# Retention heads in a decoder step: small TensorE products joined in fewer runs

## The chip, the cores and the metric

The kernel runs on one core of one Trainium2 chip, in one launch. The metric is the time of the whole launch on the device, in microseconds (us), as the median of several executions. The engines named are TensorE (PE, the matrix products; PEld is its weight load), VectorE (DVE), ScalarE (ACT), GpSimd (POOL) and SyncE (SP, which here only issues DMAs). Each runs its own program in a fixed order; semaphores make one wait for another.

## The reference, cut to what matters

One inference step of a decoder with two layers, for 512 prompt tokens and for 8 sample sequences of 4 tokens with stored states. Layer 0 is a short gated convolution, layer 1 a multi-scale retention, each followed by a gated MLP. The change lies in layer 1 alone:

```python
def step(S, qkv):
    qc, kc, vc = qkv
    scores = jnp.einsum('bhid,bhjd->bhij', qc, kc) * decay
    inner = jnp.einsum('bhij,bhjv->bhiv', scores, vc)
    cross = jnp.einsum('bhid,bhdv->bhiv', qc, S) * cross_w[:, :, None]
    S_new = S * chunk_decay[:, None, None] + jnp.einsum('bhjd,bhjv->bhdv', kc * state_w[:, :, None], vc)
    return S_new, inner + cross
...
of = (of - mu) * lax.rsqrt(var + GN_EPS)
of = of.transpose(0, 2, 1, 3).reshape(B, L, V_DIM) * gn_g.astype(jnp.float32)
out = (jax.nn.silu(g) * of.astype(x.dtype)) @ w_out
```

There are four heads, with 256 key columns and 512 value columns each. So a head has q, k (rotated) and v by projection, for the prompt and for the 32 sample tokens; the prompt's output in four tiles of 128 tokens; the samples' output, which reads a 256 x 512 state of each of the 8 sequences and writes it back updated; a normalisation over the 512 values; a gate; and an output projection.

## The kernel before, in words

Everything is in float32. A large product is made of three: each factor is split in a high and a low part (`wh`, `wl`; `xh`, `xl`), and high x high, high x low and low x high are summed in PSUM. `mm3` (L175 to L177) does this for the products of a head, `project` (L187) for projections with 272-column halves, and L1272 to L1274 for the value projection ("V products"). PSUM is handed out as two kinds of tiles: `psum()` gives one of two double banks (tag `mm`), `bank()` one of four single banks (tag `sm`). A tile that is still being read holds up the next owner of its place.

A loop over the four heads (L1575 to L1662, h = 0 to 3) does, for each head:

- `value`: 96 V products into four `sm` banks, and at two points the sample tokens' values (L1280) into the first bank of an `mm` tile, `pvs[:, 0]`. At the first of these points stand also `sample_scores` (L1462, two products of 32 columns; in head 0 one more, L1459, that turns a mask) and `keys`: eight transposes of key tiles (L1331) and two transposes of the samples' keys (L1340). Each of these three takes a `psum()` of its own. At the end of `value` the second bank, `pvs[:, 1]`, gets a product with a placing matrix (L1309).
- `state` and `scores` for the prompt, and in between `fill(n)`: pieces of the output projection of the head before (`held_project`, 48 or 24 products of L187 at a time), put there so that TensorE has work. Head 0 has none.
- `sample_outputs(i)` for the four groups i = 0 to 3: four products of 8 columns (L1493), one for each pair of sequences, that read the state tile S[i] and add into one `sm` bank, `st["po"]`. The profile shows each product as two records.
- `states_update(i)`: four products of 32 rows (L1511) into two `mm` tiles, then DVE's S update (L1516, two halves), then the store of S[i] on SP (L1518).
- `inner(it)` for the four prompt tiles it = 0 to 3 (3 to 12 `mm3` products each), and behind it `normalized`: statistics on DVE (L1404, L1405, L245/L247), a power on POOL (L248), and the normalised tile `yn` on DVE (L1408).
- `gated`: four transposes of a `yn` (L1432, on TensorE) and a multiplication of the gate by the result (L1438; L1442 for the samples, `yns`, which come from `po`). `gated_pair` does two tiles in one `mm` tile.
- `qk_project`: q and k of the next head (48 products of L187 each). In its second half, `inside()` puts update 3 and the transposes of tile 2. In head 3 a piece of `held_project` takes its place.

The order of each engine's program is made by a scheduler from the program's order and its dependencies; `tc.issue_after(x)` adds the condition that what is issued inside comes after x. It is by such conditions that groups and updates are kept behind the last product named (`last_product`).

Of the kernel before, what the change touches and what calls it, by code (L numbers as in the profile page):

```python
# [52 lines left out]
def hybrid_decode_kernel(ctx: ExitStack, tc: tile.TileContext, a: dict, o: dict):  # L53
# [1072 lines left out]
    with ExitStack() as c2:  # L1126
# [50 lines left out]
        def token_tiles(tt):  # L1177
            return slice(tt * P, (tt + 1) * P)
# [81 lines left out]
        def value(h, st):  # L1260

            pv = [bank() for _ in range(4)]
            pvs = psum()
            raw = []
            for c in range(4):
                wh, wl = load_piece(a["rtv"][h, c], 2 * DV, keep=raw)
                for k2 in range(2):
                    kt = 2 * c + k2
                    cw = slice(k2 * DV, (k2 + 1) * DV)
                    for tt in range(4):  # L1270
                        ts_, out = token_tiles(tt), pv[tt]
                        nc.tensor.matmul(out, xh[kt][:, ts_], wh[:, cw], start=(kt == 0), stop=False)  # L1272
                        nc.tensor.matmul(out, xh[kt][:, ts_], wl[:, cw], start=False, stop=False)  # L1273
                        last = nc.tensor.matmul(out, xl[kt][:, ts_], wh[:, cw], start=False, stop=(kt == KT - 1))  # L1274
                if c % 2:

                    with tc.issue_after(last.ins):
                        for g in range(4):
                            kt = 2 * c - 2 + g
                            nc.tensor.matmul(  # L1280
                                pvs[g * NS : (g + 1) * NS, 0, :], xs[:, kt, :],
                                raw[kt // 2][:, kt % 2 * DV : (kt % 2 + 1) * DV],
                                start=(c == 1), stop=(c == 3), skip_group_check=True,
                            )
                if c == 1:
                    qk_split(h, st, 1)
                    qk_split(h, st, 0)
                    gs = st["gs"] = one.tile([P, NS], F32, tag="gs", name=nm("gs"), bufs=1)
                    nc.vector.tensor_mul(
                        by_sequence(gs), by_sequence(R[:, 1, HT - NS :]), fq[:, h, :].unsqueeze(1).to_broadcast([P, NB, DS])  # L1290
                    )
                    sample_scores(h, st)
                    for dt in range(2):
                        qsrc = st["rot"][0][:, dt, SEQ:].rearrange("p (g r s) -> p g r s", g=4, r=2)
                        for r in range(2):
                            nc.vector.scalar_tensor_tensor(
                                qm[:, dt, :, r, 4 * r : 4 * r + 4], qsrc[:, :, r, :], _gamma(h) ** 4,
                                gs.rearrange("p (g r s) -> p g r s", g=4, r=2)[:, :, r, :], op0=ALU.mult, op1=ALU.mult,
                            )
                    keys(h, st)  # L1300
                    if h in AHEAD:
                        held_parts(h, older)
            v4 = tp.tile([P, 2, DV], F32R, tag="mid", name=nm("v4"), bufs=1)
            nc.scalar.activation(v4[:, 0, :], pvs[:, 0, :], AF.Copy, scale=fv[:, 4, h : h + 1])
            nc.vector.scalar_tensor_tensor(
                v4[:, 1, :], pvs[:, 0, :], fv[:, 4, h : h + 1], v4[:, 0, :].bitcast(F32), op0=ALU.mult, op1=ALU.subtract
            )
            for i in range(2):
                nc.tensor.matmul(pvs[:, 1, :], put, v4[:, i, :], start=(i == 0), stop=(i == 1))  # L1309
            vt = kp.tile([P, DV], F32R, tag="rt0", name=nm("vt"), bufs=1)  # L1310
            vs = st["vs"] = qp.tile([P, DV], F32R, tag="vs", name=nm("vs"), bufs=1)
# [12 lines left out]
            st["v"] = (vh, vl)  # L1324

        def keys(h, st):
            krot = st["rot"][1]
            pt = psum()
            for jt in range(4):
                for dt in range(2):  # L1330
                    nc.tensor.transpose(  # L1331
                        pt[:, jt // 2, (jt % 2) * 256 + dt * P : (jt % 2) * 256 + (dt + 1) * P],
                        krot[:, dt, token_tiles(jt)], ident,
                    )
            knh = tp.tile([P, 2, 512], F32R, tag="skh", name=nm("knh"), bufs=1)
            knl = tp.tile([P, 2, 512], F32R, tag="skl", name=nm("knl"), bufs=1)
            split(knh, knl, pt)
            pt = psum()
            for dt in range(2):
                nc.tensor.transpose(pt[:, 0, token_tiles(dt)], kpl[:, dt].rearrange("p g q c -> p (g q c)"), ident)  # L1340
            kns = st["kns"] = tp.tile([P, 2, 2 * P], F32R, tag="kns", name=nm("kns"), bufs=1)
            kt = tp.tile([P, 2, 2 * P], F32R, tag="rt1", name=nm("kt"), bufs=1)
            for r in range(2):
                nc.scalar.activation(kt[:, r, :], pt[:, 0, : 2 * P], AF.Copy, scale=sign[:, 2 + r : 3 + r])
            for r in range(2):
                nc.vector.scalar_tensor_tensor(
                    kns[:, r, :], pt[:, 0, : 2 * P], low_k[:, r : r + 1], kt[:, r, :].bitcast(F32),
                    op0=ALU.mult, op1=ALU.add,
                )
            st["kn"] = (knh, knl)  # L1350
# [74 lines left out]
                )  # L1425
            return pt

        def gated(h, st, yn, it, pt=None):

            pt = bank() if pt is None else pt  # L1430
            for n in range(4):
                last_product[0] = nc.tensor.transpose(pt[:, token_tiles(n)], yn[:, token_tiles(n)], ident)  # L1432
            size = 4 // len(st["gate"])
            for i, gate in enumerate(st["gate"]):
                ps_ = pt[:, i * size * P : (i + 1) * size * P]
# [7 lines left out]

        def gated_pair(h, st, *pair):
            pt = psum()
            for i, (yn, it) in enumerate(pair):
                gated(h, st, yn, it, pt[:, i, :])

        def sample_scores(h, st):

            qrot, krot = st["rot"]
            pt = psum()
            for dt in range(2):
                nc.scalar.activation(
                    kpl[:, dt, :, :3, :],
                    krot[:, dt, SEQ:].rearrange("p (g c) -> p g c", g=4).unsqueeze(2).to_broadcast([P, 4, 3, 8]), AF.Copy,
                )
            if h == 0:
                nc.tensor.matmul(pt[:, 1, :NS], put[:NS].bitcast(F32), mask_s[:NS], start=True, stop=True)  # L1459
                nc.scalar.activation(mask_put, pt[:, 1, :NS], AF.Copy)  # L1460
            for dt in range(2):
                nc.tensor.matmul(  # L1462
                    pt[:, 0, :NS], kpl[:, dt].rearrange("p g q c -> p (g q c)"), qrot[:, dt, SEQ:],
                    start=(dt == 0), stop=(dt == 1),
                )
            ss = tp.tile([P, NS], F32, tag="ss", name=nm("ss"), bufs=1)
            nc.vector.tensor_mul(ss, pt[:, 0, :NS], mask_put)
# [12 lines left out]
            S = st["S"][i] = sp.tile([P, 4, DV], F32, tag="S", name=nm("S"))  # L1480
            st["loaded"] = nc.sync.dma_start(S, rets_in[r, h, dt])

        def sample_outputs(h, st, i):


            r, dt = RD[i]
# [1 line left out]
                st["po"] = bank()  # L1488
                nc.tensor.matmul(st["po"], scp, st["vs"], start=True, stop=False, skip_group_check=True)

            with tc.issue_after(last_product[0].ins):
                for g in range(4):
                    last_product[0] = nc.tensor.matmul(  # L1493
                        st["po"][32 * g : 32 * g + 8, :], qm[:, dt, g, r, :], st["S"][i][:, g, :],
# [80 lines left out]
        for h in range(NH):  # L1575
# [30 lines left out]
            states_update(h, st, 0)  # L1606
            states_load(h, st, 3)
            fill(3)
            if h in AHEAD:
                st["gate"] = [swapped(h == 2, [P, 4, T], F32, "gate")]  # L1610
            if more:
# [10 lines left out]
                for i, t in enumerate(st["gate"]):  # L1622
                    nc.sync.dma_start(t, gate_made[h][:, 2 * i : 2 * i + 2, :])
            yn0 = normalized(inner(h, st, 0), fe[:, 0, h : h + 1])
            sample_outputs(h, st, 1)
            yn1 = normalized(inner(h, st, 1), fe[:, 1, h : h + 1])
            states_update(h, st, 1)
            if more:

# [150 lines left out]
```

## Time and profile before

| | us |
|---|---|
| median of 3 runs | 1400.66 |
| lowest and highest of them | 1400.02 to 1401.79 |
| the profiled execution's own time | 1399.59 |
| its span, from first to last instruction | 1397.8 |

The granted clock of TensorE was 0.999 of full speed in the profiled execution. The retention heads stand between about 687 and 1002 us of the span. All durations below come from the profiled execution; the parts of a page are its head (busy time of each engine), the chain of work that ended last (each step followed back to what released it; in it a run of products of one line is one row, "x8" counts its records), the timeline (every instruction, with the idle time before it in brackets), and windows (busy time in a stretch). Products on TensorE overlap, so a row of the timeline is longer than the time between two starts; in the chain the rows add up to the time that passed.

### The profile page before, as it was taken

The numbers are of one execution on the slowest core, as the hardware profiler recorded it, in microseconds if no ns is written. First come the engines' busy times: TensorE is split into PE (matmuls) and PEld (weight loads), VectorE is DVE, ScalarE is ACT, GpSimd is POOL, SyncE is SP. The second block draws the span as 40 slices with busy tenths as digits, with TensorE's granted clock in tenths as the row PEclk, the third lists the DMA queues.
The fourth block names the chain that finished last, engine by engine and source line by source line (L and its number), as shares of the span: only waits on it lengthen the run. The fifth ranks groups of instructions, "written<-read, shape, count | busy, mean of one in ns | idle before, by whom it ended". The sixth has DMA issues, their size and how long they took to land.

```text
span 1397.8 us, 26508 instructions
## 1 busy us (share of the span) xinstructions
PE 1385.4 (99%) x10433; PEld 1314.1 (94%) x10433; DVE 1131.6 (81%) x1923; ACT 824.0 (59%) x1286; POOL 219.3 (16%) x255
## 2 busy tenths in 40 slices
PE   9999999999999999999999999999999999999997
PEld 9999999999999999999977877887899999999997
DVE  6987889898989879667867586586799898989884
ACT  7666467677667657667532314224387767677654
POOL 0111011222221214111200000000112212121212
PEclk9999999999999999999999999999999999999999
DMA  6466347768686744777667355465766877777742
GB/s 207 125 165 167 108 110 159 177 163 184 145 191 150 174 114 142 189 194 202 208 215 238 121 213 181 139 242 182 211 143 154 171 176 173 155 185 154 167 105 87
DMA packets 99294, 233.68 MB, mean 167 GB/s; under 512 B 9793, under 2 KB 33489, under 8 KB 98785
## 3 DMA queue, kind: packets, MB, share of 16 engines
q1 hardware_dynamic: 68032, 167.47, 38.4%
q0 software_dynamic: 28688, 56.61, 23.6%
q10 hardware_dynamic: 2448, 7.91, 1.5%
q8 instruction: 81, 1.33, 0.4%
q14 instruction: 45, 0.36, 0.1%
HBM read 191.84 MB, written 28.42 MB: 158 GB/s over the span
## 4 chain that ended last, share of the span: by engine, by line
PE 92%; DVE 4%; DMA 1%; issue 1%; ACT 1%; POOL 0%; SPq 0%; DVEq 0%; POOLq 0%; ACTq 0%
PE sm L389 43%; PE mm L389 16%; PE mm L187 14%; PE sm L187 4%; PE sm L1272 2%; PE sm L1274 2%; PE sm L1273 2%; PE sm L175 2%; PE sm L177 2%; PE sm L176 1%; PE sm L1493 1%; DMA w<-in_cvin_dram 1%; DVE S L1516 1%; PE mm L1280 1%; PE mm L1432 1%
## 5 line engine op out<-in xcount | busy, mean ns | idle before, releaser
L389 PE MATMUL sm<-oh,wh 128*128 128x272 f32 x856 | 247.8, 290 | 0.5 <-DVE b L450 0.5
L389 PE MATMUL sm<-ol,wh 128*128 128x272 f32 x856 | 246.1, 288 | 0.0
L389 PE MATMUL sm<-oh,wl 128*128 128x272 f32 x856 | 246.1, 287 | 0.0
L202 ACT ACTIVATE h<-w 128x1024 fp32r<-128x1024 f32 (+3 forms) x170 | 136.4, 803 | 94.6 <-PE mm L389 81.2
L203 DVE TENSOR_TENSOR l<-w,h 128x1024 fp32r<-128x1024 f32 (+3 forms) x170 | 153.6, 904 | 21.4 <-ACT h L202 19.4
L318 ACT ACTIVATE wh<-w 128x1024 fp32r<-128x1024 f32 (+1 forms) x134 | 133.9, 999 | 55.9 <-PE sm L389 47.7
L389 PEld LDWEIGHTS sm<-oh,wh 128*128 128x128 f32 x856 | 161.3, 188 | 2.0 <-DVE b L450 0.9
L389 PEld LDWEIGHTS sm<-oh,wl 128*128 128x128 f32 x856 | 161.0, 188 | 0.0
L389 PEld LDWEIGHTS sm<-ol,wh 128*128 128x128 f32 x856 | 160.8, 188 | 0.1
L389 PE MATMUL sm<-parts,wh 128*128 128x272 f32 x736 | 142.5, 288 | 0.0
L202 ACT ACTIVATE wh<-w 128x1024 fp32r<-128x1024 f32 (+3 forms) x76 | 68.1, 898 | 119.9 <-PE mm L187 61.4
L321 POOL DMA_DIRECT2D wl<-in_ffgu_dram x87 | 81.7, 939 | 323.1 <-ACT wl L320 97.4
L389 PEld LDWEIGHTS sm<-parts,wh 128*128 128x128 f32 x736 | 115.4, 188 | 0.0
L389 PE MATMUL mm<-oh,h 128*128 128x272 f32 x396 | 114.0, 288 | 0.0
L389 PE MATMUL mm<-oh,l 128*128 128x272 f32 x396 | 113.4, 286 | 0.0
L389 PE MATMUL mm<-ol,h 128*128 128x272 f32 x396 | 113.1, 286 | 0.0
L319 DVE TENSOR_TENSOR wl<-w,wh 128x512 fp32r<-128x512 f32 (+1 forms) x134 | 87.3, 652 | 25.0 <-ACT wh L318 24.7
L389 PE MATMUL sm<-parts,wl 128*128 128x272 f32 x368 | 106.2, 289 | 0.2 <-DMA wl<-in_rtqk_dram 0.2
L320 ACT ACTIVATE wl<-wh 128x512 fp32r<-128x512 f32 (+1 forms) x173 | 103.0, 595 | 2.2
L203 DVE TENSOR_TENSOR wl<-w,wh 128x1024 fp32r<-128x1024 f32 (+3 forms) x76 | 80.1, 1057 | 12.4 <-ACT wh L202 11.6
L187 PE MATMUL mm<-parts,wh 128*128 128x272 f32 x488 | 82.5, 290 | 0.2 <-ACT wh L202 0.2
L389 PE MATMUL sm<-oh,h 128*128 128x272 f32 x284 | 82.3, 290 | 0.2 <-ACT oh L202 0.2
(381 smaller groups left out, 3837.1 us busy)
## 6 DMA issues: line engine op xcount, KB each, us to landing
w<-in_ffgu_dram SPq DMA_DIRECT2D x66, 512.0 KB
wl<-in_ffgu_dram POOLq DMA_DIRECT2D x87, 256.0 KB, 5.3
S<-in_rets_dram SPq DMA_DIRECT2D x16, 1024.0 KB
out_rets_dram<-S SPq DMA_DIRECT2D x16, 1024.0 KB
w<-in_ffdn_dram SPq DMA_DIRECT2D x36, 384.0 KB
cb<-in_ffgu_dram SPq DMA_DIRECT2D x22, 512.0 KB
w<-in_cvin_dram SPq DMA_DIRECT2D x21, 512.0 KB
wl<-in_ffdn_dram POOLq DMA_DIRECT2D x48, 192.0 KB, 4.7
```

Of the source, the lines that this page charges most:

```text
L175: nc.tensor.matmul(out, lh, rh, start=start, stop=False, skip_group_check=True)
L177: last_product[0] = nc.tensor.matmul(out, ll, rh, start=False, stop=stop, skip_group_check=True)
L187: last_product[0] = nc.tensor.matmul(half(pt, hf)[:, :HT], w[:, c], act[k][:, hf * HT : (hf + 1) * HT], start=(first and k == ks[0] and i ...
L202: h = nc.scalar.activation(dh, src, AF.Copy)
L203: last_low[0] = nc.vector.tensor_sub(dl, src, dh.bitcast(F32))
L318: nc.scalar.activation(wh, w, AF.Copy)
L319: last_mixed[0] = nc.vector.tensor_sub(wl[:, :n], w[:, :n], wh[:, :n].bitcast(F32))
L320: nc.scalar.activation(wl[:, n:], wh[:, n:].bitcast(F32), AF.Copy, scale=-1.0)
L321: nc.gpsimd.dma_start(wl[:, n:], src[:, 1, :] if len(src.shape) == 3 else src[:, n:], accum_op=ALU.add)
L389: last = nc.tensor.matmul(out, w[:, c], b, start=(first and j == 0 and i == 0), stop=(j == len(self.ks) - 1 and i == 2), skip_group_check= ...
L1272: nc.tensor.matmul(out, xh[kt][:, ts_], wh[:, cw], start=(kt == 0), stop=False)
L1273: nc.tensor.matmul(out, xh[kt][:, ts_], wl[:, cw], start=False, stop=False)
```

## The change

It does five things, all in the retention heads.

1. `sample_scores` and the two key transposes of the samples no longer take a `psum()` each; they write `pvs[:, 1]`, the second bank of v's tile, which is free until L1309. The scheduler then puts them and the eight key transposes directly behind L1280.
2. `sample_outputs(1)` stands behind `inner(1)` in the code, and its products are ordered behind the last product of `fill(3)`.
3. `inside()` transposes tile 2 first and then does update 3.
4. `gated` is split in `over` (the transposes) and `through` (the gate's multiplications); `gated_pair` does the eight transposes back to back, the pair's second tile first.
5. With that, the first pair (tiles 0 and 1) stands directly ahead of group 3, and the last pair (samples and tile 3) stands 22 V products (head 1: 29) behind the start of the next head's V stream; before, the samples' transposes stood at its start and tile 3's 20 products later.

```diff
-                    sample_scores(h, st)
+                    sample_scores(h, st, pvs[:, 1, :])
...
-                    keys(h, st)
+                    keys(h, st, pvs[:, 1, P:])
...
-            pt = psum()
             for dt in range(2):
-                nc.tensor.transpose(pt[:, 0, token_tiles(dt)], kpl[:, dt].rearrange("p g q c -> p (g q c)"), ident)
+                nc.tensor.transpose(placed[:, token_tiles(dt)], kpl[:, dt].rearrange("p g q c -> p (g q c)"), ident)
...
-        def gated(h, st, yn, it, pt=None):
-
-            pt = bank() if pt is None else pt
+        def over(pt, yn):
+
             for n in range(4):
                 last_product[0] = nc.tensor.transpose(pt[:, token_tiles(n)], yn[:, token_tiles(n)], ident)
+
+        def gated(h, st, yn, it):
+
+            pt = bank()
+            over(pt, yn)
+            through(st, pt, it)
...
         def gated_pair(h, st, *pair):
             pt = psum()
-            for i, (yn, it) in enumerate(pair):
-                gated(h, st, yn, it, pt[:, i, :])
-
-        def sample_scores(h, st):
+            over(pt[:, 1, :], pair[1][0])
+            with tc.issue_after(last_product[0].ins):
+                over(pt[:, 0, :], pair[0][0])
+            for i, (_, it) in enumerate(pair):
+                through(st, pt[:, i, :], it)
+
+        def sample_scores(h, st, pt):
...
-        def sample_outputs(h, st, i):
+        def sample_outputs(h, st, i, behind=None):
...
-            with tc.issue_after(last_product[0].ins):
+            with tc.issue_after(last_product[0].ins), tc.issue_after((behind or last_product[0]).ins):
...
             fill(3)
+            filled = last_product[0]
...
             yn0 = normalized(inner(h, st, 0), fe[:, 0, h : h + 1])
-            sample_outputs(h, st, 1)
             yn1 = normalized(inner(h, st, 1), fe[:, 1, h : h + 1])
+            sample_outputs(h, st, 1, filled)
             states_update(h, st, 1)
...
             def inside():
+                gated(h, st, yn2, 2)
                 states_update(h, st, 3)
-                gated(h, st, yn2, 2)
```

Lines shift by up to 10 in the changed kernel: L1493 becomes L1502, L1511 L1520, L1432 L1430, L1462 L1471, L1340 L1339, L1408 L1407.

What it does to the programs of the engines is seen at three places. First, TensorE in the second head (h = 1), around the 48 held products of L187. Before, one product of group 1 stands ahead of them and three behind, and update 1 with group 2 stands six products further on:

```order
L177 MATMUL sm_9726<-vh_9380,sl_9551 128x512
L1493 MATMUL sm_9646<-S_9392,qm 8x512
L187 MATMUL mm_9669<-oldh_9300,wh_9664 128x272 x2
...
L187 MATMUL mm_9695<-oldh_9301,wl_9665 128x272 x2
L1493 MATMUL sm_9646<-S_9392,qm 8x512 x3
L175 MATMUL sm_9743<-vh_9380,sh_9550 128x512
...
L177 MATMUL sm_9743<-vh_9380,sl_9551 128x512
L1511 MATMUL mm_9759<-vs_9377,kns_9294 128x512 x2
L1511 MATMUL mm_9760<-vs_9377,kns_9294 128x512 x2
L1493 MATMUL sm_9646<-S_9394,qm 8x512 x4
```

And now:

```order
L187 MATMUL mm_9691<-oldh_9297,wl_9661 128x272 x2
L175 MATMUL sm_9735<-vh_9376,sh_9546 128x512
L176 MATMUL sm_9735<-vl_9377,sh_9546 128x512
L177 MATMUL sm_9735<-vh_9376,sl_9547 128x512
L1502 MATMUL sm_9642<-S_9388,qm 8x512 x4
L1520 MATMUL mm_9755<-vs_9373,kns_9290 128x512 x2
L1520 MATMUL mm_9756<-vs_9373,kns_9290 128x512 x2
L1502 MATMUL sm_9642<-S_9390,qm 8x512 x4
L175 MATMUL sm_9776<-mid_9452,qkhl_9256 128x512
```

Group 1 is whole and stands with update 1 and group 2 in one run. Second, TensorE in the second head's V stream, at the first of the two points in `value`. Before:

```order
L1280 MATMUL mm_9190<-w_9221,xs 32x512 x2
L1462 MATMUL mm_9263<-rot_8908,kpl 128x32 x2
L1272 MATMUL sm_9186<-wh_9308,parts 128x512
L1273 MATMUL sm_9186<-wl_9309,parts 128x512
L1331 MATMUL mm_9278<-cb,rot_8909 128x128 x8
L1274 MATMUL sm_9186<-wh_9308,parts 128x512
...
L1272 MATMUL sm_9186<-wh_9308,parts 128x512
L1340 MATMUL mm_9291<-cb,kpl 128x128 x2
L1273 MATMUL sm_9186<-wl_9309,parts 128x512
```

And now, all of it in one run and on two `mm` tiles where there were four:

```order
L1280 MATMUL mm_9188<-w_9219,xs 32x512 x2
L1471 MATMUL mm_9188<-rot_8906,kpl 128x32 x2
L1331 MATMUL mm_9275<-cb,rot_8907 128x128 x8
L1339 MATMUL mm_9188<-cb,kpl 128x128 x2
L1272 MATMUL sm_9184<-wh_9304,parts 128x512
```

In the first head L1468 (before L1459) and three of the eight transposes stand ahead of L1471. Third, TensorE in the middle of the first head's second projection (`inside()`). Before:

```order
L187 MATMUL sm_9096<-parts,wl_9091 128x272
L1511 MATMUL mm_9121<-vs_8794,kns_8718 128x512 x2
L1511 MATMUL mm_9122<-vs_8794,kns_8718 128x512 x2
L187 MATMUL sm_9095<-parts,wh_9090 128x272
L1432 MATMUL sm_9130<-cb,yn_9069 128x128 x4
L187 MATMUL sm_9096<-parts,wh_9090 128x272
```

And now:

```order
L187 MATMUL sm_9094<-parts,wl_9089 128x272
L1430 MATMUL sm_9119<-cb,yn_9067 128x128 x4
L1520 MATMUL mm_9125<-vs_8792,kns_8716 128x512 x2
L1520 MATMUL mm_9126<-vs_8792,kns_8716 128x512 x2
L187 MATMUL sm_9093<-parts,wh_9088 128x272
```

The transposes stand first and touch the update. On DVE, in the same head, the samples' statistics now stand ahead of a weight split, their normalised tile ahead of the second half of update 2, and the normalised tile 3 behind update 3 as before. On SP only the second head's order differs: the gate's load stands ahead of the load of state tile 3 and of the next head's rotary load, where it stood behind both.

More of the change, by code (lines that the diff above doesn't have):

```diff
@@ L1324, in value, with keys @@
             st["v"] = (vh, vl)
-        def keys(h, st):
+        def keys(h, st, placed):
             krot = st["rot"][1]
@@ L1343, in keys @@
             for r in range(2):
-                nc.scalar.activation(kt[:, r, :], pt[:, 0, : 2 * P], AF.Copy, scale=sign[:, 2 + r : 3 + r])
+                nc.scalar.activation(kt[:, r, :], placed[:, : 2 * P], AF.Copy, scale=sign[:, 2 + r : 3 + r])
             for r in range(2):
                 nc.vector.scalar_tensor_tensor(
-                    kns[:, r, :], pt[:, 0, : 2 * P], low_k[:, r : r + 1], kt[:, r, :].bitcast(F32),
+                    kns[:, r, :], placed[:, : 2 * P], low_k[:, r : r + 1], kt[:, r, :].bitcast(F32),
                     op0=ALU.mult, op1=ALU.add,
@@ L1426, in inner, with through @@
             return pt
-        def gated(h, st, yn, it, pt=None):
-            pt = bank() if pt is None else pt
+        def over(pt, yn):
             for n in range(4):
                 last_product[0] = nc.tensor.transpose(pt[:, token_tiles(n)], yn[:, token_tiles(n)], ident)
+        def gated(h, st, yn, it):
+            pt = bank()
+            over(pt, yn)
+            through(st, pt, it)
+        def through(st, pt, it):
             size = 4 // len(st["gate"])
@@ L1445, in gated_pair @@
             pt = psum()
-            for i, (yn, it) in enumerate(pair):
-                gated(h, st, yn, it, pt[:, i, :])
-        def sample_scores(h, st):
+            over(pt[:, 1, :], pair[1][0])
[4 more added lines that the diff above has]
+        def sample_scores(h, st, pt):
             qrot, krot = st["rot"]
-            pt = psum()
             for dt in range(2):
@@ L1458, in sample_scores @@
             if h == 0:
-                nc.tensor.matmul(pt[:, 1, :NS], put[:NS].bitcast(F32), mask_s[:NS], start=True, stop=True)
-                nc.scalar.activation(mask_put, pt[:, 1, :NS], AF.Copy)
+                nc.tensor.matmul(pt[:, NS : 2 * NS], put[:NS].bitcast(F32), mask_s[:NS], start=True, stop=True)
+                nc.scalar.activation(mask_put, pt[:, NS : 2 * NS], AF.Copy)
             for dt in range(2):
                 nc.tensor.matmul(
-                    pt[:, 0, :NS], kpl[:, dt].rearrange("p g q c -> p (g q c)"), qrot[:, dt, SEQ:],
+                    pt[:, :NS], kpl[:, dt].rearrange("p g q c -> p (g q c)"), qrot[:, dt, SEQ:],
                     start=(dt == 0), stop=(dt == 1),
@@ L1466, in sample_scores @@
             ss = tp.tile([P, NS], F32, tag="ss", name=nm("ss"), bufs=1)
-            nc.vector.tensor_mul(ss, pt[:, 0, :NS], mask_put)
+            nc.vector.tensor_mul(ss, pt[:, :NS], mask_put)
             nc.vector.tensor_mul(ss, ss, st["gs"])
```

## The prediction

> **What bounds the kernel now.** I read the page's head first, then the shares of the chain that ended last.
>
> ```profile
> span 1397.8 us, 26508 instructions
> PE 1385.4 (99%) x10433; PEld 1314.1 (94%) x10433; DVE 1131.6 (81%) x1923; ACT 824.0 (59%) x1286; POOL 219.3 (16%) x255
> PE 92%; DVE 4%; DMA 1%; issue 1%; ACT 1%; POOL 0%; SPq 0%; DVEq 0%; POOLq 0%; ACTq 0%
> ```
>
> TensorE (PE) is busy for 1385.4 of 1397.8 us, and 92% of the chain is its own program. So there is almost no waiting to remove. A change in the order of TensorE's products can only pay if some product takes longer because of what stands before it. To see whether any does, I read the chain of waits where it runs through TensorE alone, in the second head. Its columns are the start in us, the duration in us, and the engine, PSUM kind and line.
>
> ```profile
> 807.83 0.95 PE sm L1493 x2
> 808.78 6.22 PE mm L187 x48
> 815.01 0.97 PE sm L1493 x6
> 815.98 0.43 PE sm L175
> ...
> 817.57 0.44 PE mm L1511 x3
> 818.01 0.97 PE sm L1493 x8
> 818.98 0.43 PE sm L175
> ...
> 821.26 6.02 PE mm L187 x48
> 827.29 0.44 PE mm L1432 x4
> 827.73 0.23 PE sm L175
> ...
> 828.87 0.48 PE mm L1432 x4
> 829.36 0.97 PE sm L1493 x8
> 830.33 0.43 PE sm L177
> ```
>
> Three things are to be seen. First, a group of L1493 takes 0.95 to 0.97 us whether 2, 6 or 8 records of it stand together (a product leaves two records, so 1, 3 or 4 products). A group cut in two is paid twice. Second, the first full product behind L1493 takes 0.43 where the same product elsewhere takes 0.23 (827.73). The same 0.20 stands on the 48 products of L187: 6.22 behind L1493, 6.02 behind a full product. So each separate run of such small products costs its own row and 0.20 behind it. Third, transposes (L1432) leave no such mark: 0.23 behind them. And where L1511 and L1493 stand together (817.57, 818.01), the second takes its usual 0.97 and the 0.20 comes once.
>
> The cut group appears in heads three and four as well; these are the second pieces:
>
> ```profile
> 904.29 0.97 PE sm L1493 x6
> 975.17 0.97 PE sm L1493 x6
> ```
>
> **Group 1 behind `inner(1)`.** In the second head the three runs now cost 0.95 + 0.20 (one product, then L187), 0.97 + 0.20 (three products) and 0.44 + 0.97 + 0.20 (update 1 with group 2), 3.93 together. Afterwards one run of group 1, update 1 and group 2 costs 0.97 + 0.44 + 0.97 + 0.20 = 2.58. That is 1.35 less, and 4.05 in heads two to four, where the group is cut. In the first head there is no held product and group 1 is whole; only its 0.20 goes. The sum is 4.25, all of it on TensorE's own chain. If joining saved nothing but the extra run, it would be 3 x (0.95 + 0.20) = 3.45; if each joint also hid some of the next group's start, perhaps 4.5. I take 4.25, since 817.57 to 818.98 shows such a joint at exactly this price. The move adds no operand that could be late: group 1 reads a state tile and a bank that its first product used 7 us sooner before (807.83 and 815.01). `inner(1)` now stands ahead of it, so DVE's statistics of that tile can start sooner; update 1 and its store start about 1.2 sooner too, since 0.95 + 0.20 went ahead of them.
>
> **Sample scores and key transposes in v's PSUM tile.** The chain in the second head's V stream:
>
> ```profile
> 762.97 0.99 PE mm L1280 x8
> 763.97 0.56 PE mm L1462 x4
> 764.53 0.32 PE sm L1272
> 764.85 0.24 PE sm L1273
> 765.08 0.87 PE mm L1331 x8
> ...
> 768.50 0.33 PE mm L1340 x2
> 768.83 0.24 PE sm L1273
> ```
>
> Before, L1280, L1462, L1331 and L1340 cost 0.99 + 0.56 + 0.87 + 0.33, and the V product behind L1462 costs 0.09 over 0.23: 2.84. Afterwards they are one run. The two last transposes go on at the pace of L1331 (0.87 / 8 = 0.11 each, 0.22 together), so the run is 0.99 + 0.56 + 0.87 + 0.22 = 2.64. That is 0.20 per head, 0.80 in four. In the first head L1459's product and the scores split the key transposes, two more joints of 0.09 each, so I take 0.6, with 0.1 and 0.8 as ends. A new wait comes with it: the key transposes of the samples now write the bank from which DVE reads the scores.
>
> ```profile
> 764.57 0.19 DVE L1467 TENSOR_TENSOR ss<-mm,mput 128x32 f32<-128x32 f32 x1 [4.42 <-PE mm L1462]
> ```
>
> DVE sat idle for 4.42 us before this read and did it in 0.19, so it is through about 0.25 after L1462, while the eight transposes between take 0.87. That covers it with 0.6 to spare. If DVE were still in other work then, what lies beyond the 0.6 would be paid by TensorE once per head, which is why the low end is 0.1.
>
> **Transposes of tile 2 ahead of update 3.** In the timeline and the chain of the first head:
>
> ```profile
> 742.85 0.51 PE L1511 MATMUL mm<-vs,kns 32*128 32x512 f32 x4
> 746.48 0.51 PE L1511 MATMUL mm<-vs,kns 32*128 32x512 f32 x4
> 747.47 0.66 PE L1432 MATMUL sm<-cb,yn 128*128 128x128 f32 x4 [0.15 <-DVE yn L1408]
> ...
> 742.92 0.49 PE mm L1511 x3
> 748.12 2.87 PE sm L187 x23
> ```
>
> From update 3's start to the 23 L187 behind the transposes it is 748.12 - 746.48 = 1.64, less 0.07 because the timeline starts this run 0.07 ahead of the chain (742.85 and 742.92): 1.57. Between them stands one L187 (2.87 / 23 = 0.125). Afterwards the same work is 0.48 for the transposes, 0.44 for the update, 0.20 behind it and 0.125: 1.25. The gain is 0.32, of which 0.15 is the wait for DVE's normalised samples. It needs that tile (which frees the bank the transposes write) to come earlier too, and the order on DVE does that: its statistics now stand ahead of a weight split and it stands ahead of the second half of update 2. Three heads give 0.96; the ends are 0.5 (the wait stays) and 1.4 (it also falls in heads two and three by more). In the fourth head this place lies on a chain through DVE, where I take 0:
>
> ```profile
> 997.87 0.82 DVE yn L1408
> 998.73 0.67 PE mm L1432 x4
> ```
>
> TensorE waits there for the last normalised tile whichever way the transposes ahead stand.
>
> **Pairs of transposed tiles.** First pair: before, 0.44 + 0.48 + 0.97 + 0.20 for two sets of transposes with five products between and group 3 (827.29 to 830.33). Afterwards the same rows in one run. Transposes leave no mark, so 0; the first head, whose second set took 0.1 longer, gives 0.1. Last pair: before, the samples' transposes stood at the head of the next V stream and tile 3's 20 products later, and now all eight stand 22 (second head: 29) products into it. The run is 0.88 either way. But TensorE now waits with everything behind it for both tiles, and tile 3's comes late:
>
> ```profile
> 754.92 0.81 DVE L1408 TENSOR_SCALAR yn<-sm,mv,rs 128x512 f32<-128x512 f32 x1 [0.52 <-POOL rs L248]
> 756.05 0.44 PE mm L1432 x4
> 700.00:1000.00 300.00, 299.26 (x1847) 236.73 (x1848) 211.47 (x340) 85.26 (x119) 12.21 (x21) 1.00 0.56 193
> 738.00:756.00 18.00, 17.85 (x113) 13.96 (x112) 17.14 (x30) 4.29 (x5) 1.62 (x3) 1.00 0.76 258
> ```
>
> The two last rows are windows: stretch and length, then the busy time of PE, PEld, DVE, ACT and POOL, the granted clock, the DMA share and GB/s. DVE is busy for 17.14 of the 18 us up to this place, so tile 3 is set by DVE's program. It ended at 755.7, 0.3 ahead of the transposes at 756.05. In the new order TensorE comes there at about 756.05 - 0.44 (the samples' transposes, no longer ahead) + 2 x 0.23 (two more V products) - 0.4 (tile 2 and the first pair, above) = 755.7, on the same scale, just when DVE ends. I price the whole at -0.3, with +0.1 and -1.0 as ends (0.25 in each of four heads, a third of one 0.81 DVE pass).
>
> **Moved transfers.** Only the second head's SP order differs: the gate load stands ahead of the load of state tile 3.
>
> ```profile
> 814.16 0.38 SPq L1481 DMA_DIRECT2D S<-in_rets_dram  x1
> 812.00:832.00 20.00, 20.00 (x133) 15.04 (x132) 16.05 (x26) 3.52 (x5) 1.08 (x2) 1.00 0.71 268
> ```
>
> The load is issued at 814.16 and its group starts at 829.36, 15.2 later, about 14 in the new order. The store ahead of it, the gate and the tile are 3.2 MB, 12 us at the window's 268 GB/s: hidden, so 0. If the cover were gone the group would wait up to the gate's own 1.1 MB, 4 us, so this part has an end at -1 (a quarter of it). The rotary load, one place later, feeds DVE and no product for some us.
>
> **The sum.** 4.25 + 0.6 + 0.96 + 0.1 - 0.3 = 5.6. The profiled execution took 1399.59, its span and 1.8 around it; it would take 1394.0. It lies 1.07 below the median of the runs, 1400.66, so the predicted median is 1395.1. A difference within 0.2% (2.8 us) can hardly be told from none.
>
> **The rivals.** *The joints keep their price* (0.15). Each change between full products, 8-column products and 32-row products costs what it does now, wherever it stands, and only the second piece of a cut group disappears: 3.45 from three heads, less 0.0 to 0.3 elsewhere, so about 1397.2. For it speaks that the 0.20 is seen at the end of runs only, so that what happens inside one is inferred; against it 818.01, where L1493 right behind L1511 takes no longer than behind full products. [...]
>
> *The gain is eaten by waits, no change* (0.09). Tile 3 comes some 0.8 late in each head, one DVE pass, and the scores' read costs 0.3 a head: 5.6 + 0.3 - 4 x 0.8 - 4 x 0.3 = 1.5, so 1399.2.
>
> *Slower* (0.06). The place is the joined last pair. All eight transposes and the V products behind them wait for the last pass of a DVE that is 95% busy (17.14 of 18). Without this part the gain is 5.9. It is used up when tile 3 comes 1.5 after TensorE in each of four heads, and the kernel is slower by more than 0.2% from 2.2 on. If three more passes like L1408 (0.81) came ahead of it, 2.4 late, it would be 1400.66 - 5.9 + 4 x 2.4 = 1404.4. Against it: DVE's program holds no new operation, its statistics move forward, and the two V products more add 0.46 of cover.
>
> **How the numbers follow.** The forecast gets 0.70; all its terms are rows of TensorE's own chain but for the last pair. Its own ends: with the upper ends 4.5 + 0.8 + 1.4 + 0.1 + 0.1 = 6.9, 1393.8; with the lower ends of the small parts, 4.25 + 0.1 + 0.5 - 1.0 = 3.85, 1396.8. The range takes in the first rival and 1 us of scatter at either end (the three runs shown lie from 0.6 below to 1.1 above their median): 1392.8 to 1398.3. Faster: 0.70 + 0.15 = 0.85. Same: 0.09. Slower: 0.06.
>
> **What would show it.** Right for group 1: in the second head one unbroken run of 0.97, 0.44 and 0.97 behind `inner(1)`, 0.43 on the product behind it, no L1493 beside the held L187, which take 6.02. Wrong: more than 0.97 on the second of them, or 0.20 more in between. Scores: L1280 to L1339 in about 2.65; wrong if the last two transposes name DVE's read as what they waited for. Tile 2: no idle time before L1430 inside the query projection. Last pair: no idle time over 0.3 before its eight transposes. What makes the forecast wrong most easily is TensorE idle there, on DVE's last pass, in all four heads.

## The result, and the profile after

The changed kernel takes 1399.78 us (median of 14 runs, 1397.85 to 1401.79), beside 1400.19 us for the kernel before, also in 14 runs. The ratio is 0.9994, with a 95% interval of 0.9987 to 1.0000: no difference that this measurement can tell. Forecast were 1395.1 and a range that ends at 1398.3.

The head of the changed kernel's page, and the waits of TensorE in the retention heads (in us: in total, times, longest):

```profile
span 1399.0 us, 26533 instructions
PE 1384.0 (99%) x10433; PEld 1317.1 (94%) x10433; DVE 1130.1 (81%) x1923; ACT 824.0 (59%) x1286; POOL 224.5 (16%) x255
```

```profile
PE sm L1502 <- DMA S<-in_rets_dram: 2.1, 1, 2.1
PE mm L1430 <- DVE yn L1407: 0.4, 1, 0.4
PE mm L1520 <- DVE gate L1445: 0.2, 1, 0.2
```

TensorE waited 0.5 us here before, now 2.7, and the largest part is new: group 3 of some head waits for its state tile.

This profiled execution (1401.04 us) lies 1.3 above its median. Head one began 1.4 us later than in the profile of before, 0.8 of it lost in the first 25 us, where nothing is changed. So below, next to each kernel's time stands its **stage time**: from the first L1280 of head one to one and the same L389 product about 50 us behind the last head, both by their starts in the trace of the one profiled execution. Before it is 352.6 us, after 352.4.

**The joins pay as forecast.** TensorE's timeline in the second head, and the chain in its V stream:

```profile
816.13 1.04 PE L1502 MATMUL sm<-S,qm 128*8 128x512 f32 x8
817.10 0.51 PE L1520 MATMUL mm<-vs,kns 32*128 32x512 f32 x4
817.54 1.04 PE L1502 MATMUL sm<-S,qm 128*8 128x512 f32 x8
818.52 0.50 PE L175 MATMUL sm<-mid,qkhl 128*128 128x512 f32 x1
```

```profile
763.79 1.00 PE mm L1280 x8
764.79 0.56 PE mm L1471 x4
765.35 0.91 PE mm L1331 x8
766.25 0.22 PE mm L1339 x2
766.47 0.24 PE sm L1272
```

From start to start, group 1 takes 0.97, update 1 0.44 and group 2 0.98. The V-stream run takes 1.00 + 0.56 + 0.91 + 0.22 = 2.69, where 2.64 was forecast.

**But four waits are new.** First, the chain in the last head, with the windows of that stretch:

```profile
977.36 0.26 SPq L157
977.62 0.04 issue
977.66 0.03 SPq L1490
977.69 0.04 issue
977.73 7.58 DMA S<-in_rets_dram
985.32 0.04 issue
985.36 1.04 PE sm L1502 x8
986.41 0.43 PE sm L175
...
989.81 0.43 PE sm L177
990.23 0.25 PE sm L175
```

```profile
core 0: us, PE busy (x) PEld busy (x) DVE busy (x) ACT busy (x) POOL busy (x), PEclk, DMA share, GB/s
980.00:986.00 6.00, 3.87 (x35) 3.11 (x34) 4.09 (x10) 0.00 (x0) 0.54 (x1) 1.00 0.92 308
986.00:991.00 5.00, 5.00 (x20) 3.44 (x16) 1.86 (x5) 0.00 (x0) 0.54 (x1) 0.66 0.18 66
```

The load of state tile 3 (L1490) is issued right behind a weight load (L157), is on the way for 7.6 us beside it, and group 3 stands for 2.1 us. Then the granted clock averages 0.66 over 5 us. In shorter windows it is 1.00 up to 986.7, 0.50 from there to 990.1 and 1.00 again behind 990.2, and in that stretch eight full products take up to 0.43 each where 0.23 is usual. In the kernel before the same load was issued at nearly the same time, but group 3 asked for it over 3 us later:

```profile
978.05 0.38 SPq L1481 DMA_DIRECT2D S<-in_rets_dram  x1
```

```profile
986.62 1.05 PE L1493 MATMUL sm<-S,qm 128*8 128x512 f32 x8
```

Second, DVE in the second head, where it rotates the next head's keys: after, and before.

```profile
822.03 0.16 DVE L247 TENSOR_TENSOR rs<-mv,fe 128x1 f32<-128x1 f32 x1
825.81 0.72 DVE L1236 TENSOR_TENSOR rt<-rot,sqlast 128x544 f32<-128x544 f32 x1 [3.62 <-DMA rot<-km]
...
831.50 0.68 DVE L1445 TENSOR_TENSOR gate<-gate,mm 128x512 f32<-128x512 f32 x1
```

```profile
822.63 0.72 DVE L1236 TENSOR_TENSOR rt<-rot,sqlast 128x544 f32<-128x544 f32 x1
...
829.39 0.69 DVE L1438 TENSOR_TENSOR gate<-gate,mm 128x512 f32<-128x512 f32 x1
```

DVE stands idle for 3.62 us until the rotary keys are there. So its gate products, which free the first pair's `mm` tile, end 2 us later, and update 2, which needs that tile, is cut in two on TensorE:

```profile
831.64 0.49 PE L1520 MATMUL mm<-vs,kns 32*128 32x512 f32 x2
832.32 0.49 PE L1520 MATMUL mm<-vs,kns 32*128 32x512 f32 x2 [0.19 <-DVE gate L1445]
832.74 0.77 PE L187 MATMUL sm<-parts,wh 128*128 128x272 f32 x4
```

Third, the first held product of that head begins 0.24 late behind the product ahead (0.47 from start to start instead of 0.23). The `mm` tile that it writes is freed by update 0's state update, and this stands on DVE behind a weight split:

```profile
808.71 0.39 PE L177 MATMUL sm<-vh,sl 128*128 128x512 f32 x1
809.18 0.52 PE L187 MATMUL mm<-oldh,wh 128*128 128x272 f32 x2
```

```profile
806.77 1.23 DVE L203 TENSOR_TENSOR wl<-w,wh 128x1024 fp32r<-128x1024 f32 x1 [0.17 <-ACT wh L202]
807.91 2.35 DVE L1525 SCALAR_TENSOR_TENSOR S<-S,mm 128x1024 f32<-128x1024 f32 x2
```

Before, one product of group 1 (0.95 + 0.20) stood between update 0 and the held products. Fourth, the joined last pair waits 0.4 in the last head, ahead of 999.07.

**The account.** For every run of small products I took the time from the end of the full product ahead to the start of the second one behind, less one full product, in both traces, and summed by part over the four heads (us; positive is gained):

| part | forecast | trace |
|---|---|---|
| group 1 in one run | 4.25 | 4.23 |
| scores and key transposes | 0.6 | 0.54 |
| tile 2 ahead of update 3 | 0.96 | 1.31 |
| pairs | -0.2 | -0.16 |
| group 3 of the last head: pause, slow products behind | 0 | -2.19, -1.57 |
| first held products | 0 | -0.93 |
| update 2 in heads two and three | 0 | -0.92 |
| sum | 5.6 | 0.3 |

The stage times differ by 0.2. Each trace is one execution: with TensorE and DVE in the same order, update 2's run takes 1.30 and 0.88 in heads two and three here, and 1.42 and 1.70 in load_first below.

### The profile page after: what moved, and what is told of

Its sections match the earlier page's. It is cut to its first block, busy times and chain, and to the rows that moved or that the text cites. A ratio compares the mean times of both kernels' runs of the same rounds, so it can differ in the third digit from the quotient of the medians.

```text
span 1399.0 us, 26533 instructions
## 1 busy us (share of the span) xinstructions
PE 1384.0 (99%) x10433; PEld 1317.1 (94%) x10433; DVE 1130.1 (81%) x1923; ACT 824.0 (59%) x1286; POOL 224.5 (16%) x255
## 4 chain that ended last, share of the span: by engine, by line
PE 89%; DVE 4%; DMA 3%; ACT 1%; issue 1%; POOL 0%; SPq 0%; DVEq 0%; POOLq 0%; ACTq 0%
PE sm L389 43%; PE mm L389 16%; PE mm L187 12%; PE sm L187 5%; PE sm L1272 2%; PE sm L1274 2%; PE sm L1273 2%; PE sm L175 1%; PE sm L176 1%; PE sm L177 1%; DMA S<-in_rets_dram 1%; DMA rot<-km 1%; DVE S L1525 1%; PE mm L1280 1%; PE sm L1502 0%
## 5 line engine op out<-in xcount | busy, mean ns | idle before, releaser
L389 PE MATMUL sm<-oh,wh 128*128 128x272 f32 x856 | 247.8, 290 | 0.5 <-DVE b L450 0.5
L389 PE MATMUL sm<-ol,wh 128*128 128x272 f32 x856 | 246.1, 288 | 0.0
L389 PE MATMUL sm<-oh,wl 128*128 128x272 f32 x856 | 246.0, 287 | 0.0
L389 PEld LDWEIGHTS sm<-oh,wh 128*128 128x128 f32 x856 | 161.4, 188 | 2.0 <-DVE b L450 0.9
L389 PEld LDWEIGHTS sm<-oh,wl 128*128 128x128 f32 x856 | 161.0, 188 | 0.0
L389 PEld LDWEIGHTS sm<-ol,wh 128*128 128x128 f32 x856 | 160.8, 188 | 0.1
L389 PE MATMUL sm<-parts,wh 128*128 128x272 f32 x736 | 142.5, 288 | 0.0
L389 PEld LDWEIGHTS sm<-parts,wh 128*128 128x128 f32 x736 | 115.5, 188 | 0.0
L389 PE MATMUL mm<-oh,h 128*128 128x272 f32 x396 | 114.0, 288 | 0.0
L389 PE MATMUL mm<-oh,l 128*128 128x272 f32 x396 | 113.4, 286 | 0.0
L389 PE MATMUL mm<-ol,h 128*128 128x272 f32 x396 | 113.1, 286 | 0.0
L389 PE MATMUL sm<-parts,wl 128*128 128x272 f32 x368 | 106.2, 289 | 0.5 <-DMA wl<-in_rtg_dram 0.3
L187 PE MATMUL mm<-parts,wh 128*128 128x272 f32 x488 | 83.2, 292 | 0.1
L389 PE MATMUL sm<-oh,h 128*128 128x272 f32 x284 | 82.3, 290 | 0.3 <-ACT oh L202 0.2
```

Of the source, the lines that this page charges most:

```text
L187: last_product[0] = nc.tensor.matmul(half(pt, hf)[:, :HT], w[:, c], act[k][:, hf * HT : (hf + 1) * HT], start=(first and k == ks[0] and i ...
L389: last = nc.tensor.matmul(out, w[:, c], b, start=(first and j == 0 and i == 0), stop=(j == len(self.ks) - 1 and i == 2), skip_group_check= ...
```

## The experiments

Each is compared with the kernel before on the same chip, in three series: 1400.33 us for the first four, 1400.49 for the next four and 1400.55 for the last two. The quotient of two medians differs from the ratio, which is taken from all runs, by up to 0.0004. The kernels have 5 to 11 runs each, and the series stand on two chips, so a difference of less than about 1 us between two of these kernels is not told apart from their scatter. A stage time is that of one execution.

| kernel | median, us | ratio to before (95%) | stage, us |
|---|---|---|---|
| load_first | 1397.15 | 0.9974 (0.9965 to 0.9984) | 349.4 |
| apart_last_head | 1398.56 | 0.9986 (0.9977 to 0.9994) | 350.7 |
| group1_only | 1400.07 | 0.9995 (0.9986 to 1.0003) | 351.6 |
| without_group1 | 1398.94 | 0.9987 (0.9978 to 0.9997) | 351.1 |
| rotary_first | 1395.69 | 0.9965 (0.9952 to 0.9977) | 348.4 |
| split_later | 1396.31 | 0.9966 (0.9954 to 0.9978) | 348.3 |
| both_moves | 1396.37 | 0.9966 (0.9954 to 0.9979) | 347.6 |
| pairs_apart | 1398.47 | 0.9986 (0.9977 to 0.9995) | 350.2 |
| before_loads | 1400.38 | 1.0002 (0.9993 to 1.0011) | 352.5 |
| group1_loads | 1397.04 | 0.9976 (0.9967 to 0.9985) | 349.5 |

**load_first.** One weight load of the last head queued behind the load of state tile 3. Only SP's order differs from the changed kernel's.

```diff
                 if n >= 6:
-                    held_project(h, n, False)
+                    with tc.issue_after(st["loaded"].ins):
+                        held_project(h, n, False)
```

> The changed kernel with one weight load queued behind the load of state tile 3 on SP in the last head, instead of ahead of it. Theory A (the gain was spent on waits, the largest being group 3 in the last head: 2.2 us for its state tile and 1.7 us of slower products behind the pause): the tile lands 0.7 to 2 us sooner, the wait falls under 0.5 us, and the time is 1.5 to 3.9 us under the changed kernel's. Theory B (the last head ends on DVE's chain anyway, so what group 3 waits is hidden): less than 1 us under the changed kernel's.

Measured 1397.15, 2.6 under the changed kernel's 1399.78. SP's timeline and TensorE's in the last head:

```profile
976.30 0.38 SPq L1490 DMA_DIRECT2D S<-in_rets_dram  x1
```

```profile
982.85 1.04 PE L1502 MATMUL sm<-S,qm 128*8 128x512 f32 x8
983.83 0.50 PE L175 MATMUL sm<-mid,qkhl 128*128 128x512 f32 x1
984.16 0.40 PE L176 MATMUL sm<-mid,qkhl 128*128 128x512 f32 x1
```

The load no longer stands in line behind a weight load that itself waits for a buffer (4.8 us in the changed kernel), group 3 waits for nothing, and the products behind it have their usual pace (0.24 from the second to the third, at a granted clock of 1.00). The stage is 3.0 shorter and not 3.8, mainly since in this execution update 2 takes 0.9 more in heads two and three (above). Theory A holds for its largest wait; theory B, that what group 3 waits is hidden by DVE's chain, falls here: the last pair waits 0.4 as it did.

**apart_last_head.** The last head's first pair as before the change; `gated_pair_apart` does four transposes and the gate products for each tile in turn.

```diff
-                gated_pair(h, st, (yn0, 0), (yn1, 1))
+                (gated_pair if more else gated_pair_apart)(h, st, (yn0, 0), (yn1, 1))
```

> The changed kernel, but in the last head the first pair's transposes stand as before: four, six products, four, then group 3. Theory A: group 3 is asked for 1.4 us later, waits 0.8 us instead of 2.2 and slows less behind it; 1.4 to 3.5 us under the changed kernel's time. Theory B: within 1 us of it.

Measured 1398.56, 1.2 under the changed kernel: a little less than expected, and a little more than theory B allows. Group 3 now waits 0.4 in its profile, and the granted clock averages 0.998 over that execution (0.997 in the changed kernel's). But the last pair of the same head waits longer for DVE:

```profile
997.17 1.06 PE L1430 MATMUL mm<-cb,yn 128*128 128x128 f32 x8 [1.49 <-DVE yn L1407]
```

In the changed kernel it waits 0.42. So 1.1 us of what group 3 gains is lost again on DVE's chain; theory B holds for that part, and with 1.2 us the run does not decide between the two.

**group1_only.** The kernel before with the move of group 1 alone (`sample_outputs(1)` behind `inner(1)`, ordered behind `filled`, as in the change's diff).

> The kernel before with the move of group 1 alone. Theory A (the joins pay as worked out, 4.25 us, less 0.9 us that the first held products wait for the update before them; no wait for state tile 3): 3.3 us under the time before, 2.8 to 3.8. Theory C (joined runs save nothing of note, the 4 us were an artefact of how rows are read): within 1 us of the time before.

Measured 1400.07, 0.3 under the time before instead of 3.3. The joined runs are there (2.59 in its trace, as in the changed kernel), so theory C does not follow. But theory A's small price for the waits was wrong; TensorE's waits in the retention heads of its trace:

```profile
PE mm L1432 <- DVE gate L1438: 1.2, 2, 0.7
PE sm L1493 <- DMA S<-in_rets_dram: 0.8, 1, 0.8
PE sm L1432 <- DVE yn L1408: 0.3, 2, 0.2
```

With this part alone, group 3 of the last head already asks for its tile 0.8 too soon, and the first pair's second transposes wait for DVE. The trace is that of an execution of 1397.88 us, one of three from 1397.65 to 1398.53; the other eight lie from 1399.58 to 1400.83. Its stage is 1.0 shorter than before; what the other eight add is not in it.

**without_group1.** The changed kernel with group 1 back ahead of `inner(1)`.

```diff
-            yn1 = normalized(inner(h, st, 1), fe[:, 1, h : h + 1])
-            sample_outputs(h, st, 1, filled)
+            sample_outputs(h, st, 1)
+            yn1 = normalized(inner(h, st, 1), fe[:, 1, h : h + 1])
```

> The changed kernel with group 1 back ahead of inner(1). Theory A: loses the 4.25 us of the joins, but group 3 in the last head comes about 1.2 us later and waits about 1 us instead of 2.2, and the first held products wait no more: 0.5 to 2.5 us above the changed kernel's time. Theory C: no slower than the changed kernel, if anything faster, since only waits differ.

Measured 1398.94, 0.8 under the changed kernel where 0.5 to 2.5 above it was expected; the stage is 1.3 shorter. So theory A's sum was wrong, and the time is what theory C asked for; what speaks against C is the joined rows above and group1_loads below. In the profile, of the four waits only the last pair's 0.4 is left, the one for state tile 3 is gone altogether. By the account above, taking out 4.2 us of joins and 5.6 us of waits leaves 1.4 in favour. The other parts by themselves are worth 1.4 (ratio 0.9987), as their forecast said: 0.6 + 0.96 - 0.2 = 1.36.

**rotary_first.** On top of load_first: in the first three heads SP loads the next head's rotary keys first, then state tile 3, then the gate.

```diff
-            states_load(h, st, 3)
+            if not more:
+                states_load(h, st, 3)
             fill(3)
...
-                nc.sync.dma_start(nxt["rot"][1], k_made[h + 1])
+                turned_load = nc.sync.dma_start(nxt["rot"][1], k_made[h + 1])
+                with tc.issue_after(turned_load.ins):
+                    states_load(h, st, 3)
             if h in AHEAD:
-                nc.sync.dma_start(st["gate"][0], gate_made[h])
+                with tc.issue_after(turned_load.ins):
+                    nc.sync.dma_start(st["gate"][0], gate_made[h])
```

> As load_first (1397.15 us), and in the first three heads the next head's rotary keys are loaded ahead of state tile 3 and the gate on SP. Theory D (in heads two and three DVE's chain waits for the rotary keys' transfer, so update 2 waits 0.8 to 1.1 us for an mm tile that DVE still reads): the rotation starts 2 us sooner or more, update 2's run is 0.63 us again, 1.0 to 1.9 us under load_first. Rival E (DVE's own work fills the stretch, so it is no sooner done): 0.4 us under load_first at most.

Measured 1395.69, 1.5 under load_first. DVE in the second head, and the only kind of wait of TensorE in the four:

```profile
821.01 0.72 DVE L1236 TENSOR_TENSOR rt<-rot,sqlast 128x544 f32<-128x544 f32 x1
```

```profile
PE mm L1430 <- DVE yn L1407: 0.9, 3, 0.4
```

The rotation starts 4.8 us sooner than in the changed kernel and without a pause, and update 2's run takes 0.62 in both heads (1.42 and 1.70 in load_first). Theory D holds and E falls. The scheduler also moved the last pair in these two heads, to 18 V products behind the start of the stream instead of 29 and 22. Its run takes 1.31 and 1.30 there, 1.02 and 1.08 in load_first, so about 0.25 in each head is lost again.

**split_later.** On top of load_first: a weight split on DVE behind update 0 (in heads two and three; `update0` is set to update 0's last half).

```diff
             with tc.issue_after(v2_split[0].ins) if dt else ExitStack():
-                parted()
+                with tc.issue_after(update0[0].ins) if dt and h > 1 else ExitStack():
+                    parted()
```

> As load_first, and in heads two and three a weight split of 1.2 us on DVE is queued behind update 0's two halves instead of ahead of them. Theory D2 (the first held product waits 0.35 us in each of these heads for update 0, which waits for that split): the excess of 0.24 and 0.11 at the first held product goes, 0.5 to 0.8 us under load_first. Rival: the split is needed soon itself, and its delay costs as much: within 0.3 us of load_first.

Measured 1396.31, 0.8 under load_first. DVE and TensorE:

```profile
806.59 2.35 DVE L1526 SCALAR_TENSOR_TENSOR S<-S,mm 128x1024 f32<-128x1024 f32 x2 [0.92 <-PE mm L1521]
```

```profile
807.54 0.40 PE L176 MATMUL sm<-vl,sh 128*128 128x512 f32 x1
807.86 0.52 PE L187 MATMUL mm<-oldh,wh 128*128 128x272 f32 x2
```

Update 0's state update starts 0.54 us behind the start of its products (806.05) instead of 0.92 (806.99 in the changed kernel), and the first held product starts 0.32 behind the product ahead, which is 0.09 late instead of 0.24. One product fewer stands ahead of it in this order. In the third head it is 0.12 late, where it was 0.24 in load_first. That makes 0.27 in the two heads: the direction is D2's, but not the size. Most of the 1.1 us by which the stage is shorter than load_first's stands at update 2 of the third head, which takes 0.62 here and 1.70 there; whether the split's new place did that is not shown.

**both_moves.** The edits of rotary_first and split_later together.

> rotary_first and split_later together. Theories D and D2: the two gains add up, 1.5 to 2.7 us under load_first, 4.7 to 5.9 us under the time before. Rival E: less than 0.7 us under load_first.

Measured 1396.37: 0.8 under load_first instead of 1.5 to 2.7, and no better than either alone. The stage time is the shortest of all, 347.6, but five runs with a scatter of 2.7 us don't separate the three. In its trace transposes of tile 2 wait 0.2 each in heads two and three for DVE. Whether the two gains add stays open.

**pairs_apart.** On top of load_first: both pairs apart in all heads, as before the change.

```diff
-                gated_pair(h, st, (yn0, 0), (yn1, 1))
+                gated_pair_apart(h, st, (yn0, 0), (yn1, 1))
...
-            gated_pair(h, st, (yns, 4), (yn3, 3))
+            gated_pair_apart(h, st, (yns, 4), (yn3, 3))
```

> As load_first, with the transposes of both pairs apart in all heads, as before the change. If joining the pairs costs and saves nothing by itself: within 0.5 us of load_first. If it is the joined first pair that makes update 2 wait in heads two and three (its gate products come later on DVE): up to 2 us under load_first.

Measured 1398.47, 1.3 above load_first: neither expectation. With the pairs apart, the second transposes of the first pair, and group 3 behind them, wait for DVE's gate products, 1.7 us in two heads. Update 2's run does take only 0.73 and 0.62 there, but the run with the second transposes and group 3 takes 2.73 and 2.72 where it took 1.66 before the change. So where the pair stands decides at which product TensorE waits for DVE in these heads; joined, it waits no longer than apart.

**before_loads.** The kernel before with the order of loads of rotary_first (both diffs).

> The kernel before with the order of loads of rotary_first (one weight load behind state tile 3 in the last head; rotary keys ahead of state tile 3 in the others), TensorE's order untouched. If those loads only take away waits that the change brought: within 0.7 us of the time before, since there TensorE waits for none of them. If they are a gain of their own: 2 us or more under the time before.

Measured 1400.38, ratio 1.0002: the loads are worth nothing to the kernel before. Their gain above is the removal of waits that the change brought.

**group1_loads.** group1_only with that order of loads.

> group1_only with that order of loads. Theories A and D: the waits for state tile 3 (0.9 us in the last head) and of the first pair for DVE (0.7 and 0.9 us in heads two and three) go, the first held products still wait: 2 to 3.3 us under the time before, where group1_only was 0.3 under it. If the joins themselves save nothing: within 1 us of the time before.

Measured 1397.04, 3.5 under the time before, 0.2 beyond the expected end. The joined group 1, worth 0.3 us with the old order of loads, is worth 3.5 with the new one. Against before_loads, which has the same loads without the move, it is 3.3: the 4.2 of the joins less the 0.9 of the first held products.

## Why the prediction was wrong

*Its terms for TensorE were right.* Group 1 was forecast at 4.25 and is 4.23, the scores 0.6 and 0.54, the pairs -0.2 and -0.16; tile 2 ahead of update 3 was 0.96 and is 1.31, because the last head gained there too, where I had taken 0. group1_loads shows the same in measured time: 3.3 us beside the same loads, where TensorE waits neither for a load nor for the first pair.

*The joints are free.* The rival by which they keep their price is not borne out for this run: 0.97, 0.44 and 0.98 from start to start, where the rows of before have 0.97, 0.44 and 0.97, and a gain of 4.23 where that rival had 3.45. Extra time is seen only where a full product follows, the 0.20; what takes it, no run here shows.

*The step that failed is "Moved transfers", and with it "Pairs".* I wrote "Only the second head's SP order differs" and priced the rest of SP at nothing. But a transfer need not move to become late; it is enough that its reader comes sooner. In the last head the load of state tile 3 was issued at 978.05 before and 977.7 after, while group 3 came from 986.62 to 983.2, drawn forward by the joined group 1 and by the first pair, which I had priced at 0 from rows that hold no load. By the trace's transfer records the tile was there at 984.9 before, 1.7 us ahead of its use; that cover was spent. Counted from the start of head one, group 3 was asked for 4.8 sooner, but the load, behind its weight load, was issued only 1.7 sooner. I tested such a cover for the second head's load alone, and not in the last, where a weight load stands ahead in the queue. This wait and the slow products behind it cost 3.8 of the 5.6.

*"The rotary load, one place later, feeds DVE and no product for some us"* was the second error. DVE's idle time was read as slack. DVE hands back the `mm` tiles of the first pair, so its delay of 2 us reached TensorE at update 2. In the third head SP's order is as before, and DVE still waits 2.6 for its rotary keys in load_first where it waited 0.5 before the change: there too the reader comes sooner. That is 0.9 us in the two heads; rotary_first gave it back.

*The first held products* were not thought of. I looked for what each removed run costs and not for what it covered: the one product of group 1 ahead of the held ones covered update 0's state update on DVE. That is 0.9.

*The last pair* costs about what it was priced at (-0.3). Its one pause over the 0.3 that the prediction named as a sign, 0.42, stands in the last head and not in all four. The slower rival, all on this pair, did not come. The rival "the gain is eaten by waits" named the right outcome with other waits, at 0.09.

## What to carry to other kernels

One engine carried 92% of the chain here, and what the joins take off its own time was summed from its rows almost to the tenth (group 1: 4.25 forecast, 4.23 in the trace). But what was taken out brought the readers nearer to their transfers and to the engine that frees their buffers: group 3 of the last head came 3.4 us sooner and stood for 2.1. So before summing, list for each load, and for each buffer that comes back from another engine, when it is there and when it is asked for, in every repetition of the loop, and compare that slack with the sum of what is removed ahead of it. A removed piece of work may have been the cover of something else, and the order of loads is then part of the change: here the same loads in another order were worth nothing before it and 4 us after.

## What the runs showed that was not expected

A pause of 2.13 us on TensorE was followed by 3.4 us at a granted clock of 0.50 (986.7 to 990.1), which cost another 1.6 us. The clock fell 1.3 us behind the end of the pause, when group 3 was already through. In load_first, without the pause, it is 1.00 from 980 to 991. The pause of 1.5 us in apart_last_head left the products behind it at their pace: the clock is 1.00 from 996 to 1002, and from 998.58 on two products of 272 columns start every 0.25 us, as they did ahead of it. In group1_only, where the longest pause is 0.8, the clock averages 0.999 over the execution, as before the change. So the pause of 2.1 us cost nearly twice its length here, and the one of 1.5 its length alone; one execution shows each. The longer one stood behind 1.0 us of transposes and ahead of 1.0 us of 8-column products; what made the clock fall, no run here shows.
